# Taking the modulation's steps two together at every second place of a two-layer diffusion trunk

## The chip, the cores and the metric

The kernel runs on one core of one Trainium2 chip. The time is that of the device, in microseconds (us), for one execution; the median of several runs is compared.

## What is computed

Two layers of a diffusion trunk over 512 latent and 256 context tokens of 1024 features, all in 32-bit floats. Each layer has a SwiGLU block, a block of four parallel mixers, and a second SwiGLU block. Before and after each block the stream is scaled and shifted by vectors that depend on the condition alone, the modulation: nine vectors of 1024 values a layer and condition.

```python
m_l = (jax.nn.silu(c) @ w_mod[l] + b_mod[l]).reshape(b, N_MOD, d).transpose(1, 0, 2)[:, :, None, :]
m_c = (jax.nn.silu(c_ctx) @ w_mod[l] + b_mod[l]).reshape(N_MOD, 1, 1, d)

h_lat = h_lat + 0.5 * m_l[2] * swiglu(modulate(rms_norm(h_lat, g_ffn1[l]), m_l[0], m_l[1]),
                                      w1_gate[l], w1_up[l], w1_down[l])
z_lat = split_in(modulate(rms_norm(h_lat, g_mix[l]), m_l[3], m_l[4]) @ w_in[l])
...
h_lat = h_lat + m_l[5] * (jnp.concatenate([o_a, o_b, o_c, o_d], axis=-1) @ w_out[l])
h_lat = h_lat + 0.5 * m_l[8] * swiglu(modulate(rms_norm(h_lat, g_ffn2[l]), m_l[6], m_l[7]),
                                      w2_gate[l], w2_up[l], w2_down[l])
```

The context tokens (h_ctx, with m_c) go through the same blocks up to the last layer's mixers.

## The kernel before

Features lie on the 128 partitions and tokens on the free axis; the stream `h` stays on the chip (8 tiles of 128 features, 768 tokens). Every product is done in three passes on operands that are split into a high and a low part (`mm3`, L162: weights low by tokens high, high by low, high by high). A weight block of 128 x 512 comes from the memory into one of four `raw` buffers (`load`, L152, on SyncE's queue, SP) and is split by a ScalarE copy (L133) and a VectorE subtraction (L134) into `wh` and `wl` (`unit`).

The two SwiGLU blocks of a layer (`ffn`) go through the 22 hidden tiles in six chunks of 4, 2, 4, 4, 4 and 4. The first chunk is done by plain products (`first_pairs`, `plain`), the others by Strassen-Winograd over pairs of hidden tiles (`gate_up`: 7 products of 12 matmuls for the gate, m = 0, then 7 for the up part, m = 1). After a chunk's hidden tiles its part of the down product is added to `h` (`down`). Between them lie the mixers (`mixer`): input projection, two convolutions, and an attention stage that runs as a pipeline over units (scores and softmax, transposed weights, values), and then the output projection (`out_proj`).

The modulation is computed as filler between these products. `mod_group` is a generator for four blocks of 256 columns of `w_mod`. Its step k loads row block k (128 rows, 1024 columns, 512 KB) into the next of two buffers `mraw` (L176) and multiplies it with the 32 columns of `sc`, which hold silu of the two conditions (L179: four products of 128 x 32 by 128 x 256, each into its own 32 partitions of the bank `pmod`). After the eighth step ScalarE copies the sums (L184), TensorE transposes them twice (L186), and VectorE adds the bias (L195). The first two groups run at the start, from 16 buffers of their own (`i`). The other 16 groups, 128 steps, stand in `self.filler`. `fill(n)` takes n steps; it is called

- in the SwiGLU blocks of layer 0 (`FILLS`, L50, is 1 there and 0 in layer 1): after each gate or up half of a plain hidden tile (L371), after a hidden tile of the first pair (L400), before each half of a Strassen pair (L458), and after each chunk (L579). The call after a chunk and that before the next chunk's first half follow each other with no product between them;
- once for each unit of the attention pipeline (L1026) and for each column tile of the output projection (L1056), in both layers;
- by `need` and by the first chunk's end, if a part of the modulation is wanted that is not there yet (L209, L532).

I call each such call a place. The order on each engine's queue is set by the framework's scheduler, which takes the program's order with some parts moved ahead (`rise`); it may put other instructions between those of a step.

Of the kernel before, what the change touches and what calls it, by code (L numbers as in the profile page):

```python
# [33 lines left out]
# column tiles of the input projection, in order  # L34
T_CFA, T_CFG, T_KV, T_QA, T_QB, T_WQ, T_WK, T_WV, T_SC = 0, 2, 4, 5, 16, 6, 8, 9, 10

# small per-layer vectors: name -> (offset, width)
# [9 lines left out]
class K:  # L47
# [9 lines left out]
    def __init__(self, tc, ctx, a, out):  # L57
        self.tc, self.nc, self.a, self.out = tc, tc.nc, a, out
        self.const = ctx.enter_context(tc.tile_pool(name="const", bufs=1))
        psum = ctx.enter_context(tc.tile_pool(name="psum", bufs=1, space=bass.MemoryType.PSUM))  # L60
        ct = self.ct
        self.raw = deque(ct(f"raw{i}", (P, 1024)) for i in range(self.N_RAW))
        self.mraw = deque(ct(f"mraw{i}", (P, 1024)) for i in range(self.N_MRAW))
        self.wr = deque((ct(f"wh{i}", (P, 512), F32R), ct(f"wl{i}", (P, 512), F32R)) for i in range(self.N_W))
        # PSUM: two banks, and six that each phase cuts for itself
        self.mod_ps = psum.tile([P, 512], F32, name="pmod")
        self.one = psum.tile([P, 512], F32, name="pone")
        self.filler, self.found, self.open = iter(()), set(), False
        self.n = 0
# [4 lines left out]
    # ---- buffers: handed out and given back in program order  # L74
# [4 lines left out]
    @contextmanager  # L79
    def area(self, name, side="left"):  # L80
        """A phase's buffers: each in a pool of its own, so that it waits only for the users of its own bytes."""
        with ExitStack() as st:
            def take(n, w, dt=F32):
                ts = deque()
                for _ in range(n):
                    u = self.uid(name)
                    pool = st.enter_context(self.tc.tile_pool(name=u, bufs=1, side=side, reuse_waits="tile"))
                    ts.append(pool.tile([P, w], dt, name=u))
                return ts
            yield take  # L90

    def psum(self, st, n, w):
        """n pieces of PSUM, each in a pool of its own."""
        ts = deque()
        for _ in range(n):
            u = self.uid("ps")
            pool = st.enter_context(self.tc.tile_pool(name=u, bufs=1, space=bass.MemoryType.PSUM, reuse_waits="tile"))
            ts.append(pool.tile([P, w], F32, name=u))
        return ts
# [19 lines left out]
    def rise(self, n):  # L119
        """Work that the scheduler is to take as if it came n instructions earlier."""  # L120
        return self.tc.high_priority(n) if n else nullcontext()
# [5 lines left out]
    # ---- exact two-part split: x = hi + lo, each of 12 significant bits  # L127
# [13 lines left out]
    def unit(self, src, neg=False):  # L141
        """A split [parts, <= 512] block of weights."""
        hi, lo = self.turn(self.wr)
        p, w = src.shape[0], src.shape[-1]
        hi, lo = hi[:p, :w], lo[:p, :w]
        with self.rise(self.P_UNIT):
            self.split(hi, lo, src, neg)
        return hi, lo
# [6 lines left out]
    def mm3(self, ps, w, x, start, stop):  # L155
        """ps += w^T x for split operands, each [K, M] / [K, N]; N is cut at PSUM's banks."""
# [7 lines left out]
    # ---- modulation vectors  # L164
    def mod_group(self, l, blocks):
        """Two pairs of neighbouring blocks of 256 columns of silu(c) @ w_mod, for both conditions; one step a row block."""
# [39 lines left out]
    def need(self, l, part):  # L206
        """Has what is left of a part of the modulation computed."""
        while not {(l, 4 * part + j) for j in range(4)} <= self.found:
            self.fill()  # L209
# [5 lines left out]
    def norm_gain(self, l, part, ks=(0, 4)):  # L215
        """g * (1 + scale), both conditions."""
# [15 lines left out]
    # ---- norms  # L232
    def segs(self, a, b):
        """Token range [a, b) by condition."""
        return [(i, max(a, s), min(b, e)) for i, (s, e) in enumerate(((0, SEQ), (SEQ, TOK))) if max(a, s) < min(b, e)]

    def sumsq(self, k, a, b):
        """Adds the squares of h[k] to the running sum of this norm."""
# [10 lines left out]
    def sums(self, ps, tiles, n):  # L249
        """The sum over partitions and tiles, on all partitions."""  # L250
# [6 lines left out]
    def rsqrt(self, out, x, scale):  # L257
        """1 / sqrt(scale * x + eps)"""
# [3 lines left out]
    def spread(self, ps, rc):  # L262
        """A row of values by token on all partitions, from columns of values by token."""
# [3 lines left out]
    def inv_rms(self, ps, tiles, n, scale, j0=0):  # L267
        """1 / sqrt(scale * sum of squares + eps) on all partitions (in PSUM), found by token."""
# [9 lines left out]
    def rnorm(self, a, b, ps=None):  # L278
        """1 / rms(h) for tokens [a, b), on all partitions (in PSUM)."""
# [3 lines left out]
    def modulated(self, hi, lo, t, k, r, gain, l, part, a, b):  # L283
        """hi + lo = h[k] * gain * r + shift for tokens [a, b)."""
# [14 lines left out]
    # ---- SwiGLU. The gate and up products go by Strassen-Winograd over two column tiles,  # L299
    # two halves of the features and two halves of the tokens.  # L300
    def token_operands(self, X, hn, r, gain, l, part, half, kk):
        """Half of the features of the modulated norm of half of the tokens, split: B11 and B21, or B12 and B22."""
# [7 lines left out]
    def token_sums(self, X, hn):  # L310
        """T1 = B12 - B11, T2 = B22 - T1, T3 = B22 - B12, T4 = T2 - B21, split."""
# [24 lines left out]
    def half_load(self, idx, rs, f, m, kk):  # L336
        """Half of the features of the gate's (m = 0) or the up product's (m = 1) column tile f."""
# [8 lines left out]
    def whole(self, ps, w, x, hn, start, stop):  # L346
        """ps += a whole product over half of the features."""
# [4 lines left out]
    def hidden(self, g, j, hn, pss):  # L352
        """silu(gate) * up, split, for half j of the tokens."""
# [8 lines left out]
    def plain(self, idx, f, X, g, hn, fills):  # L362
        """The split hidden tile f by plain products."""
        pss = [[self.banks.popleft() for _ in range(2)] for _ in range(2)]
        for m in range(2):
# [5 lines left out]
            self.fill(fills)  # L371
# [3 lines left out]
    def first_pairs(self, idx, X, g, hn, norm, operands, fills, start):  # L375
        """The first four hidden tiles by plain products, while the operands are being made."""
# [16 lines left out]
        def product(f, j, kk):  # L393
# [4 lines left out]
            if kk == 1:  # L398
                self.hidden(g[f], j, hn, (pss[f, 0, j], pss[f, 1, j]))
                self.fill(fills)  # L400

        steps = self.STEPS if start else ((0, 0, (0, 1), ()), (0, 1, (), (0, 1)), (1, 0, (0, 1), ()), (1, 1, (), (0, 1)))
        for j, kk, lower, upper in steps:
            if kk == 0:
                r[j] = norm(j)
                if start and j == 0:
                    # both halves' norms are in use at a time
# [16 lines left out]
    def gate_up(self, idx, f, X, g, hn, fills):  # L424
        """g[0], g[1]: the split hidden tiles f and f + 1."""
# [11 lines left out]
        def ready(m, i, j, c):  # L437
            """c: tile i, token half j of the gate (m = 0) or up (m = 1) product."""
# [18 lines left out]
        for m, M in enumerate(mats):  # L457
            self.fill(fills)  # L458
# [35 lines left out]
    def ffn(self, l, which, part, n, cuts, fills, start=None):  # L494
        """cuts: token ranges in which the last chunk is finished;
        start: for the first of all, what gives the norms, and the weights that have been loaded."""
# [3 lines left out]
        with ExitStack() as st:  # L500
# [18 lines left out]
            for ci, nf in enumerate(F_CHUNKS):  # L519
# [18 lines left out]
                def down(i, w, j0, ranges):  # L538
                    """Column tile i over token ranges; w: its weights from column j0 on."""
# [36 lines left out]
                else:  # L576
                    if ci == 0:
                        self.token_sums(X, hn)
                    self.fill(fills)  # L579
                f0 += nf  # L580

    # ---- rotary embedding on partitions [p0, p1), latent tokens
# [14 lines left out]
    def dw_conv(self, y, u, w, taps, bias, segs):  # L597
        """y[t] = bias + sum_j w[:, j] u[t + j - taps // 2], zeros outside of each segment."""
# [18 lines left out]
    # ---- the four mixers; returns the 8 split tiles that the output projection reads  # L617
    def mixer(self, l, n, st):
        """n: tokens whose output is wanted (TOK, or SEQ in the last layer)."""
# [11 lines left out]
        # modulated norm, by stream  # L631
# [9 lines left out]
        def proj_parts(tiles, ranges, m=P):  # L641
            """Column tiles of the input projection, token range by token range."""
# [18 lines left out]
        # conformer: u = a * sigmoid(g), then a depthwise convolution spread over the other projections  # L661
# [18 lines left out]
        # kv latent  # L680
# [8 lines left out]
        # q latent (two tiles) and the shared rotary key  # L689
# [8 lines left out]
        # 1 / rms of the q latent, by token  # L698
# [14 lines left out]
        # window q, k, v  # L713
# [14 lines left out]
        # ---- attention  # L728
# [21 lines left out]
        # attention runs as a pipeline over units: scores and softmax; transposed weights; values  # L750
        po = self.one

        def transposed(blocks, res):
            """blocks: pairs of [128, 128] sources; [128, 512] split tiles of two pairs each."""
# [12 lines left out]
        # windowed attention with sink: units of 128 queries and one key head (two query heads)  # L767
# [6 lines left out]
        class Window:  # L774
# [6 lines left out]
            def softmax(w):  # L781
# [20 lines left out]
                # -max(scale * scores, sink)  # L802
# [31 lines left out]
        # latent attention: units of 256 queries of a head  # L834
# [48 lines left out]
        def mla_query(ps, c, m, wa, wb):  # L883
            """Columns [c, c + m) of the query projection."""
# [3 lines left out]
        def mla_rotary(h, wa, wb):  # L888
            """The rotary parts of the queries of heads h and h + 1, split, in rows that the query latent leaves free."""
# [42 lines left out]
        def window_operands():  # L932
            # a head's two parts above each other: one product sums two passes
# [27 lines left out]
        # short conv: b * conv(c * x); the first head of the latent attention starts beside it  # L961
# [35 lines left out]
        for i in range(len(units) + lv):  # L997
# [28 lines left out]
            self.fill()  # L1026
# [8 lines left out]
    def out_proj(self, l, o, gate, n):  # L1035
# [5 lines left out]
        def part(i, ranges):  # L1041
# [14 lines left out]
            self.fill()  # L1056
# [31 lines left out]
    def run(self, ctx):  # L1088
        nc, a, ct = self.nc, self.a, self.ct
        # constants and small vectors  # L1090
# [29 lines left out]
        with self.area("i") as init:  # L1120
            # keeps the place of the next phase's first buffers
# [42 lines left out]
        # final norm  # L1164
# [46 lines left out]
def _lay(inp):  # L1211
    """Layout only: transposes, permutations and packing of the inputs."""
# [3 lines left out]
    def fm(v):  # [n] -> [128, n/128]  # L1216
        return np.ascontiguousarray(v.reshape(-1, P).T)

    def lhs(w):  # [L, K, M] -> [L, M/128, 128, (K/128)*128]: one block per column tile
# [10 lines left out]
    # down projections: [128, chunk][column tile][row tile][128]  # L1230
# [6 lines left out]
    # input projection: columns by tile  # L1237
# [8 lines left out]
    # query projection: the heads' plain parts, then their rotary parts  # L1246
# [43 lines left out]
```

## Time and profile before

| | |
|---|---|
| median of 3 runs | 2734.28 us (2730.88 to 2735.37) |
| profiled execution, span from its first to its last instruction | 2729.7 us |
| profiled execution, time outside the span | not given apart; the median of the runs is 4.6 us above the span |
| TensorE busy | 2687.2 us (98% of the span) |
| VectorE, ScalarE, GpSimd busy | 1998.7, 1108.8, 65.5 us |
| transfers | 254.83 MB, 93 GB/s on average |
| modulation steps in the filler | 128 loads of 512 KB, 1024 matmul records on L179 |

Of the span, about 50 to 590 us are layer 0's first SwiGLU, up to 750 the head of its mixers, up to 905 its attention, up to 985 its output projection, up to 1500 its second SwiGLU. Layer 1 has its first SwiGLU up to 2050, its mixers up to 2316, its output projection up to 2360 and its second SwiGLU to the end.

How to read it: PE is TensorE's matmul, PEld its weight load, DVE VectorE, ACT ScalarE, POOL GpSimd, SPq SyncE's queue, which issues the loads. Matmul records have modelled ends and overlap, so the distance from one start to the next tells what a product costs, not the duration of its record. A product of 32-bit operands that are not rounded (L179) shows as two records.

### The profile page before, as it was taken

What the parts mean: (1) busy time and instruction counts of PE and PEld (TensorE: products, weight loads), DVE (VectorE), ACT (ScalarE), POOL (GpSimd) and SP (SyncE); (2) the same over time, 40 slices, a digit from 0 to 9 for tenths busy, and PEclk for the clock granted to TensorE, in tenths of its full rate; (3) what the DMA queues carried; (4) which work ended last, traced back from release to release, by engine and by line L of the source; (5) the groups of instructions that cost most, each with busy time, mean ns of one, the idle gap of its engine ahead of it and who ended that gap; (6) DMA issues with size and microseconds to landing.
All of it is one profiled execution on the core that took longest, in us unless ns stands there. A gap on an engine that the chain in (4) does not pass through costs nothing.

```text
span 2729.7 us, 41155 instructions
## 1 busy us (share of the span) xinstructions
PE 2687.2 (98%) x16292; PEld 2458.7 (90%) x16292; DVE 1998.7 (73%) x3884; ACT 1108.8 (41%) x2096; POOL 65.5 (2%) x88
## 2 busy tenths in 40 slices
PE   7999999999999999999999999999999999999998
PEld 5999999988876899999999999999998877899998
DVE  5777666779785476767667867776678785698887
ACT  4333323343375342333234523343244375444444
POOL 0000000000022000000000000000000021000000
PEclk9999999999999999999999999999999999999999
DMA  7323222321123342323223132222222122423322
GB/s 269 108 101 100 79 96 90 108 83 57 55 78 93 109 139 93 101 93 103 83 85 124 48 100 70 63 79 60 63 85 99 58 78 78 138 94 98 104 93 78
DMA packets 78241, 254.83 MB, mean 93 GB/s; under 512 B 8672, under 2 KB 14048, under 8 KB 77792
## 3 DMA queue, kind: packets, MB, share of 16 engines
q1 hardware_dynamic: 78048, 252.21, 28.7%
q8 instruction: 127, 2.08, 0.3%
q14 instruction: 66, 0.54, 0.1%
HBM read 250.08 MB, written 2.10 MB: 92 GB/s over the span
## 4 chain that ended last, share of the span: by engine, by line
PE 94%; DVE 4%; DMA 1%; ACT 1%; issue 1%; POOL 0%; DVEq 0%; SPq 0%; POOLq 0%; ACTq 0%
PE ps L162 73%; PE pone L162 10%; PE pmod L179 3%; PE pmod L162 3%; PE ps L595 1%; PE ps L793 1%; PE ps L798 1%; DVE r L134 0%; DMA raw<-in_w_gu 0%; DVE sm L852 0%; PE ps L796 0%; DMA mraw<-in_w_mod 0%; DVE wl L134 0%; PE ps L272 0%; PE pone L272 0%
## 5 line engine op out<-in xcount | busy, mean ns | idle before, releaser
L162 PE MATMUL ps<-x,wh 128*128 128x384 f32 (+1 forms) x3064 | 748.9, 329 | 0.0
L162 PEld LDWEIGHTS ps<-x,wh 128*128 128x128 f32 x3064 | 542.7, 188 | 0.1
L162 PE MATMUL ps<-x,wl 128*128 128x384 f32 (+1 forms) x1532 | 506.1, 331 | 0.0
L133 ACT ACTIVATE wh<-raw 128x512 fp32r<-128x512 f32 (+1 forms) x445 | 278.3, 626 | 486.9 <-PE ps L162 336.3
L134 DVE TENSOR_TENSOR wl<-raw,wh 128x512 fp32r<-128x512 f32 (+1 forms) x445 | 305.2, 687 | 121.9 <-ACT wh L133 119.1
L162 PE MATMUL ps<-t,wh 128*128 128x384 f32 (+2 forms) x1488 | 385.2, 341 | 0.3 <-DVE t L134 0.3
L162 PE MATMUL ps<-r,wh 128*128 128x512 f32 (+7 forms) x1432 | 355.5, 350 | 0.3 <-DVE r L291 0.3
L296 DVE SCALAR_TENSOR_TENSOR h<-ps,hg,h 128x256 f32<-128x256 f32 (+3 forms) x404 | 186.8, 506 | 186.6 <-PE ps L162 186.1
L162 PEld LDWEIGHTS ps<-x,wl 128*128 128x128 f32 x1532 | 287.6, 188 | 12.9 <-issue 10.7
L162 PEld LDWEIGHTS ps<-t,wh 128*128 128x128 f32 x1488 | 269.2, 188 | 7.2 <-DVE t L134 0.5
L133 ACT ACTIVATE wh<-t 128x512 fp32r<-128x512 f32 x217 | 136.0, 629 | 337.1 <-PE ps L162 201.9
L162 PEld LDWEIGHTS ps<-r,wh 128*128 128x128 f32 (+3 forms) x1432 | 236.4, 184 | 36.1 <-DVE r L291 1.5
L450 DVE TENSOR_TENSOR t<-t,ps 128x384 f32<-128x384 f32 (+1 forms) x422 | 217.2, 520 | 52.6 <-PE ps L162 50.2
L162 PE MATMUL ps<-t,wl 128*128 128x384 f32 (+2 forms) x744 | 253.4, 342 | 1.6 <-ACT t L133 1.6
L162 PE MATMUL ps<-r,wl 128*128 128x512 f32 (+5 forms) x716 | 225.1, 355 | 2.4 <-ACT r L290 1.3
L134 DVE TENSOR_TENSOR wl<-t,wh 128x512 fp32r<-128x512 f32 x217 | 149.1, 689 | 95.2 <-ACT wh L133 95.0
L133 ACT ACTIVATE t<-t 128x384 fp32r<-128x384 f32 (+2 forms) x247 | 130.2, 536 | 208.9 <-DVE t L444 100.7
L162 PE MATMUL ps<-x,t 128*128 128x384 f32 (+1 forms) x1308 | 204.4, 310 | 0.0
L162 PEld LDWEIGHTS ps<-x,t 128*128 128x128 f32 x1308 | 194.4, 188 | 0.0
L162 PE MATMUL ps<-t,t 128*128 128x384 f32 (+2 forms) x948 | 188.9, 345 | 0.0
L162 PEld LDWEIGHTS ps<-t,t 128*128 128x128 f32 x948 | 165.5, 188 | 10.9 <-issue 1.2
L134 DVE TENSOR_TENSOR t<-t,t 128x384 fp32r<-128x384 f32 (+2 forms) x247 | 137.4, 568 | 25.4 <-ACT t L133 25.0
(215 smaller groups left out, 3711.0 us busy)
## 6 DMA issues: line engine op xcount, KB each, us to landing
raw<-in_w_gu SPq DMA_DIRECT2D x160, 512.0 KB, 3.8
mraw<-in_w_mod SPq DMA_DIRECT2D x128, 512.0 KB, 4.0
raw<-in_w_dn SPq DMA_DIRECT2D x88, 512.0 KB, 3.7
raw<-in_w_in SPq DMA_DIRECT2D x34, 512.0 KB, 3.3
raw<-in_w_out SPq DMA_DIRECT2D x20, 512.0 KB, 3.4
i<-in_w_mod SPq DMA_DIRECT2D x32, 256.0 KB, 6.0
raw<-in_w_gu SPq DMA_DIRECT2D x32, 256.0 KB, 3.5
h<-in_h SPq DMA_DIRECT2D x4, 768.0 KB, 6.6
```

The costliest lines, as they stand in the source:

```text
L133: self.nc.scalar.activation(hi, x, AF.Copy)
L134: self.nc.vector.tensor_tensor(out=lo, in0=x, in1=hi.bitcast(F32), op=ALU.subtract)
L162: self.nc.tensor.matmul(ps[:, c:e], a, b[:, c:e], start=start and i == 0, stop=stop and i == 2)
L179: nc.tensor.matmul(ps[32 * j:32 * j + 32, :256], self.sc[:, k, :], r[:, j * 256:(j + 1) * 256], start=k == 0, stop=k == KD - 1)
L296: nc.vector.scalar_tensor_tensor(out=self.h[:, k, s:e], in0=ps[:, s - a:e - a], scalar=gate[:, k, i:i + 1], in1=self.h[:, k, s:e], op0=ALU ...
L450: eng.tensor_tensor(out=out, in0=p, in1=q, op=op)
L595: self.nc.tensor.transpose(out, in_, self.ident)
L793: nc.tensor.matmul(ps[:, c0:SEQ], a, b[:, kc], start=i == 0, stop=False)
L798: nc.tensor.matmul(ps[:, SEQ:TOK], a, b[:, SEQ:], start=i == 0, stop=i == 1)
```

## The change

A new function `spot` takes the place of `fill` at all places named above but `need` and the first chunk's end: it notes the steps owed and takes them when two or more have come together. So the first of two places does nothing and the second takes two steps. With `FILLS` 0 nothing is owed.

```diff
-        self.filler, self.found, self.open = iter(()), set(), False
+        self.filler, self.found, self.open, self.owed = iter(()), set(), False, 0
...
     def fill(self, n=1):
         for _ in range(n):
             next(self.filler, None)
 
+    def spot(self, n=1):
+        self.owed += n
+        if self.owed > 1:
+            self.fill(self.owed)
+            self.owed = 0
...
     def plain(self, idx, f, X, g, hn, fills):
...
-            self.fill(fills)
+            self.spot(fills)
...
     def first_pairs(self, idx, X, g, hn, norm, operands, fills, start):
...
-                self.fill(fills)
+                self.spot(fills)
...
     def gate_up(self, idx, f, X, g, hn, fills):
...
-            self.fill(fills)
+            self.spot(fills)
...
     def ffn(self, l, which, part, n, cuts, fills, start=None):
...
-                    self.fill(fills)
+                    self.spot(fills)
...
     def mixer(self, l, n, st):
...
-            self.fill()
+            self.spot()
...
     def out_proj(self, l, o, gate, n):
...
-            self.fill()
+            self.spot()
```

The lines below `spot` have numbers higher by 7 in the changed kernel: L162 is L169 there, L179 L186, L176 L183, L152 L159.

How the order on the queues moves is shown at three places. In the names, `x` are token operands, `wl` and `wh` split weights, `ps` and `pone` banks of sums, `mraw_65` and `mraw_66` the two buffers of the modulation, `sc` the condition.

**TensorE, layer 0's first SwiGLU, fourth chunk.** Before, at the border between the gate half and the up half of the chunk's first pair, and at the border to its second pair:

```order
L162 MATMUL ps_382<-x_530,wh_67 128x384
L162 MATMUL ps_382<-x_526,wh_67 128x384
L179 MATMUL pmod<-mraw_65,sc 32x256 x4
L162 MATMUL ps_390<-x_486,wl_70 128x384
L162 MATMUL ps_390<-x_490,wh_69 128x384
```

```order
L162 MATMUL ps_382<-x_530,wh_69 128x384
L162 MATMUL ps_382<-x_526,wh_69 128x384
L179 MATMUL pmod<-mraw_66,sc 32x256 x4
L162 MATMUL ps_390<-x_486,wl_72 128x384
L162 MATMUL ps_390<-x_490,wh_71 128x384
```

Now, at the same two borders:

```order
L169 MATMUL ps_382<-x_526,wl_68 128x384
L169 MATMUL ps_382<-x_530,wh_67 128x384
L169 MATMUL ps_382<-x_526,wh_67 128x384
L169 MATMUL ps_390<-x_486,wl_70 128x384
L169 MATMUL ps_390<-x_490,wh_69 128x384
```

```order
L169 MATMUL ps_382<-x_530,wh_69 128x384
L169 MATMUL ps_382<-x_526,wh_69 128x384
L186 MATMUL pmod<-mraw_65,sc 32x256 x4
L186 MATMUL pmod<-mraw_66,sc 32x256 x4
L169 MATMUL ps_390<-x_486,wl_72 128x384
```

The first border has no step any more, and the second has both, one behind the other.

**SP's queue, the loads around the same chunk** (`in_w_gu` gate and up weights, `in_w_dn` down weights). Before:

```order
L152 DMA raw_63<-in_w_gu 128x1024
L176 DMA mraw_66<-in_w_mod 128x1024
L176 DMA mraw_65<-in_w_mod 128x1024
L152 DMA raw_64<-in_w_gu 128x1024
L152 DMA raw_61<-in_w_gu 128x1024
L176 DMA mraw_66<-in_w_mod 128x1024
L152 DMA raw_62<-in_w_gu 128x1024
L152 DMA raw_63<-in_w_dn 128x1024
L176 DMA mraw_65<-in_w_mod 128x1024
L152 DMA raw_64<-in_w_dn 128x1024
L152 DMA raw_61<-in_w_dn 128x1024
L176 DMA mraw_66<-in_w_mod 128x1024
```

Now:

```order
L159 DMA raw_63<-in_w_gu 128x1024
L183 DMA mraw_65<-in_w_mod 128x1024
L183 DMA mraw_66<-in_w_mod 128x1024
L159 DMA raw_64<-in_w_gu 128x1024
L159 DMA raw_61<-in_w_gu 128x1024
L183 DMA mraw_65<-in_w_mod 128x1024
L183 DMA mraw_66<-in_w_mod 128x1024
L159 DMA raw_62<-in_w_gu 128x1024
L159 DMA raw_63<-in_w_dn 128x1024
L159 DMA raw_64<-in_w_dn 128x1024
L159 DMA raw_61<-in_w_dn 128x1024
L183 DMA mraw_65<-in_w_mod 128x1024
```

The weight loads have kept their order; two modulation loads now stand together between them where there was one at each of two points.

**TensorE, layer 0's attention stage, windowed units** (`f` and `r` are attention operands, `ident` the identity of a transpose). Before, two places in a row:

```order
L595 MATMUL ps_6337<-ident,f_4941 128x128
L179 MATMUL pmod<-mraw_65,sc 32x256 x4
L162 MATMUL pone<-f_4872,r_5033 64x256
L162 MATMUL pone<-f_4884,r_5029 64x256
L162 MATMUL pone<-f_4872,r_5029 64x256
```

```order
L798 MATMUL ps_5069<-r_4997,r_5053 128x256
L162 MATMUL pone<-f_4880,r_5029 64x256
L179 MATMUL pmod<-mraw_66,sc 32x256 x4
L595 MATMUL ps_6333<-ident,f_4953 128x128
L595 MATMUL ps_6337<-ident,f_4953 128x128
```

Now:

```order
L602 MATMUL ps_6332<-ident,f_4936 128x128
L186 MATMUL pmod<-mraw_65,sc 32x256
L169 MATMUL pone<-f_4867,r_5028 64x256
L169 MATMUL pone<-f_4879,r_5024 64x256
L169 MATMUL pone<-f_4867,r_5024 64x256
```

```order
L805 MATMUL ps_5064<-r_4992,r_5048 128x256
L169 MATMUL pone<-f_4875,r_5028 64x256
L186 MATMUL pmod<-mraw_65,sc 32x256 x3
L186 MATMUL pmod<-mraw_66,sc 32x256 x4
L602 MATMUL ps_6328<-ident,f_4948 128x128
```

Here the scheduler has put the first product of the pair's first step at the earlier point, and the other seven at the later one.

## Rows read from the trace of the kernel before

**Rows 1.** The page: engine totals, and the chain that ended last by engine.

```profile
PE 2687.2 (98%) x16292; PEld 2458.7 (90%) x16292; DVE 1998.7 (73%) x3884; ACT 1108.8 (41%) x2096; POOL 65.5 (2%) x88
...
PE 94%; DVE 4%; DMA 1%; ACT 1%; issue 1%; POOL 0%; DVEq 0%; SPq 0%; POOLq 0%; ACTq 0%
```

**Rows 2.** Windows: stretch, its length, each engine's busy time, clock, DMA share, GB/s.

```profile
50.00:560.00 510.00, 510.00 (x3021) 490.83 (x3020) 364.08 (x690) 177.99 (x324) 0.00 (x0) 1.00 0.31 99
750.00:912.00 162.00, 158.52 (x1070) 114.94 (x1070) 108.12 (x246) 105.95 (x239) 35.75 (x48) 0.99 0.28 85
1615.00:2050.00 435.00, 435.00 (x2461) 433.01 (x2460) 310.63 (x572) 148.99 (x266) 0.00 (x0) 1.00 0.23 69
2190.00:2316.00 126.00, 123.38 (x800) 91.14 (x801) 88.42 (x188) 82.63 (x180) 28.96 (x32) 0.99 0.23 72
```

**Rows 3.** TensorE's timeline (start, us, records) around one step, layer 0's second SwiGLU.

```profile
1253.61 0.34 PE L162 MATMUL ps<-x,wl 128*128 128x384 f32 x1
...
1254.14 0.34 PE L162 MATMUL ps<-x,wl 128*128 128x384 f32 x1
1254.32 0.52 PE L162 MATMUL ps<-x,wh 128*128 128x384 f32 x2
1254.77 0.64 PE L179 MATMUL pmod<-mraw,sc 128*32 128x256 f32 x8
1255.33 0.45 PE L162 MATMUL ps<-x,wl 128*128 128x384 f32 x1
...
1255.97 0.34 PE L162 MATMUL ps<-x,wl 128*128 128x384 f32 x1
```

**Rows 4.** TensorE's timeline around two steps at a border between chunks, same stage.

```profile
1238.14 0.69 PE L162 MATMUL ps<-t,t 128*128 128x384 f32 x3
1238.75 1.07 PE L179 MATMUL pmod<-mraw,sc 128*32 128x256 f32 x16
1239.75 0.44 PE L162 MATMUL ps<-x,wl 128*128 128x384 f32 x1
...
1240.39 0.34 PE L162 MATMUL ps<-x,wl 128*128 128x384 f32 x1
```

**Rows 5.** TensorE's timeline at two points of layer 0's attention stage.

```profile
865.82 0.95 PE L162 MATMUL pone<-f,r 128*64 128x256 f32 x6
866.70 0.64 PE L179 MATMUL pmod<-mraw,sc 128*32 128x256 f32 x8
867.27 0.44 PE L595 MATMUL ps<-ident,f 128*128 128x128 f32 x2
...
890.58 1.05 PE L179 MATMUL pmod<-mraw,sc 128*32 128x256 f32 x10
891.56 0.70 PE L798 MATMUL ps<-r,r 128*128 128x256 f32 x2
```

**Rows 6.** Waits of 750 to 912 us: engine, line, for whom; us, times, longest.

```profile
PE ps L162 <- ACT f L855: 1.6, 2, 1.3
```

**Rows 7.** Waits of SP's queue over the whole span.

```profile
SPq L152 <- DVE t L450: 881.1, 90, 18.8
...
SPq L176 <- PE pmod L179: 498.4, 110, 19.8
```

**Rows 8.** TensorE's timeline, end of layer 0's output projection and the next stage's start.

```profile
978.85 0.64 PE L179 MATMUL pmod<-mraw,sc 128*32 128x256 f32 x8
...
983.85 1.07 PE L179 MATMUL pmod<-mraw,sc 128*32 128x256 f32 x16
985.45 0.58 PE L162 MATMUL ps<-x,x 128*128 128x384 f32 x2 [0.53 <-ACT x L290]
```

**Rows 9.** Modulation loads, issue to landing: two issued together (1093 us); one alone (1255 us).

```profile
DMA to landing us min/median/max: 4.1/4.9/5.8
...
mraw<-in_w_mod SPq DMA_DIRECT2D x1, 512.0 KB, 4.3
```

## Prediction

> **What bounds the kernel now.** I read the totals and the chain of waits first. TensorE is busy for 2687.2 of 2729.7 us and the chain that ended last runs through it for 94% [rows 1]. The windows by stage then tell where it has slack. In the first SwiGLU stage it is busy in every one of 510.00 us, in the second layer's first SwiGLU in 435.00 of 435.00, in the two attention stages in 158.52 of 162.00 and 123.38 of 126.00 [rows 2]. The granted clock is 1.00 (2.4 GHz) or 0.99 in them. So a microsecond taken out of TensorE's queue in these stages is a microsecond off the end, and the question is what one modulation step takes out of that queue, alone and behind another.
>
> The timeline has both forms in the kernel as it is. A place (where the filler is called) with **one step** shows as 8 records (4 products of two records each); where the end of a chunk and the start of the next stand side by side, two steps already come together, as 16 records. I call an unbroken stretch of modulation products on TensorE a **visit**.
>
> - One step: the products around it come in threes (one with the low weights, two with the high ones), and a three takes 1254.14 - 1253.61 = 0.53 us. Around the visit two threes take 1255.97 - 1254.14 = 1.83 us in place of 1.06, so the visit costs **0.77 us** [rows 3].
> - Two steps together: three products start at 1238.14 and the next would start at 1238.67; it starts at 1239.75, 1.08 late, and the three behind it takes 0.64 in place of 0.53, 0.11 more. The visit costs **1.19 us** [rows 4].
>
> Two visits of one step cost 1.54 us, one visit of two costs 1.19: **0.35 us less for each visit that goes away**. What is dear is going in and coming out (the gap before the first record, the longer way to the next product and its slow start), not the step, which adds 1.19 - 0.77 = 0.42.
>
> **The change, part by part.** *How many visits go.* The number of steps stays 128. Counted in the two orders that are printed, the steps of these 16 groups make 128 visits before (a coincidence: some hold two steps, and the scheduler cuts others into pieces) and 91 after. By stage, before and after: SwiGLU 1 of layer 0 28 and 17; its attention 31 and 25; its output projection 10 and 5; SwiGLU 2 26 and 16; the stretch into layer 1 5 and 5; layer 1's mixer head 4 and 4, attention 18 and 16, output projection 6 and 3.
>
> *SwiGLU and output projections: 11 + 5 + 10 + 3 = 29 visits.* Both sides of a visit are the 384- or 512-column products of rows 3 and 4, so 29 x 0.35 = **10.2 us**. The inside of a chunk goes from three visits to one or two; the double at every border between chunks stays, so the place where hidden tiles and down products meet keeps what it has.
>
> *Attention: 6 + 2 = 8 visits.* The neighbours are short products and transposes. A step of 8 records takes 0.57 us from its first record to the next product (866.70 to 867.27), 10 records of two steps take 0.98 (890.58 to 891.56) [rows 5]. Two visits of 0.57 against one of 0.98 is 0.16 saved at least; with the gap on going in, as in rows 3, up to 0.35. I take 0.25, since transposes stand nearer together than the products of rows 3 and lose less: 8 x 0.25 = **2.0 us**, with 1.3 and 2.8 as ends.
>
> *Places that lose their step.* About half of the places have nothing now, and the next half tile's products come 0.77 us sooner. Its weights must be split by then (ScalarE, then VectorE). The nearest row is layer 1's first SwiGLU, the same code with no step at any place: TensorE idles for nothing in 435 us [rows 2]. I cost it at 0 there. In the attention stages such a place may leave a wait open that a step covered; the largest wait on the softmax's exponentials is 1.6 us in two times [rows 6]. I cost it at 0 and keep 0 to 5 us for the range.
>
> *The loads.* Each step loads a row block of 512 KB into one of two buffers, on SP's queue, and that load waits until the step two before it has been multiplied. SP already waits 498.4 us for that, 110 times, and 881.1 us in one group alone for weight buffers [rows 7]. Both buffers of a pair now come free together, so two loads go out behind each other, once for two places, with the weight loads behind them. Set against the times of before, no weight load then stands behind a modulation load whose buffer frees later than that weight load went out anyway: weight buffers hold SP longer. The tightest pair is the end of layer 0's output projection: one visit at 978.85, the next at 983.85 [rows 8], with two loads between them where there was one. Two loads issued together landed after 4.1 and 5.8 us, one alone after 4.3 [rows 9]. So the second may come up to 1.5 us late; TensorE waits 0.53 us for ScalarE right behind this visit [rows 8], which hides part. I cost it at **0.5 us**, with 0 and 1.5 as ends.
>
> On this one place the Trainium skill speaks against the change: by "Trainium Kernel Development and Optimization", section Key Constraints, all transfers run on the same 16 DMA engines and interleave, so two loads at once should each take about twice as long. At 2 x 4.3 = 8.6 us the wait would be some 4 us and the sum 8.2 in place of 11.7; the trace's 5.8 us for the later of a pair agrees only in part.
>
> *Elsewhere.* VectorE, ScalarE and GpSimd have the same operations. No part of the modulation comes later than it is wanted: pairs end with their groups of 8 steps, and each group closes within a few products of where it did.
>
> **The sum.** 10.2 + 2.0 - 0.5 = 11.7 us off the profiled span of 2729.7, so 2718.0. The three timed runs have a median 4.6 us above that span (2734.28); I take that distance to stay: **2722.6 us**, 0.43% faster. About 0.2% (5.5 us) is what a measurement of this kernel can tell from no change.
>
> **Rivals.**
> - *Attention gives it back* (2728.8 to 2739). Some 18 places there lose their step. If at each the softmax chain leaves TensorE waiting as long as a visit took (0.57), 10.3 us return and 2733 is left. For it: these are the only stages with idle time, and the scheduler puts their products in another order. Against it: the named wait is 1.6 us [rows 6]. Within 0.2%, 13%.
> - *Slower: the weights come late behind pairs.* The later load of a pair lands 5.8 - 4.1 = 1.7 us after the first [rows 9], and a weight load behind both lands later by as much. In the two SwiGLU stages of layer 0 some 31 visits are pairs; if TensorE waited 1.7 us at the 20 new ones, that is 34 us, and 2722.6 + 34 = 2757. It decides as soon as a weight's lead, from landing to its first split, is under 1.7 us; half of that wait is enough for no gain. Against it: the 11 doubles of now have weight loads behind them too, and TensorE does not idle there [rows 2]. 7%.
> - *The pairs don't come about.* The scheduler may take steps apart, as it does in attention, where a first product goes ahead and the other seven follow. If nothing is gained there the time is 2724.6, inside the forecast's range.
> - *Less of a saving than the double shows*, because it stands at a border between chunks: with 0.16 (rows 5) at all 37 the gain is 5.9, less 0.5, and the time 2728.9. 5%, 2 of them faster and 3 no change.
>
> **Chances and range.** The forecast 75%, the rivals 13, 7 and 5%: so faster 75 + 2 = 77%, no measurable change 13 + 3 = 16%, slower 7%. The forecast's own range: 29 x 0.35 + 2.8 = 13.0 off at best gives 2721.3, and runs spread over 4.5 us, so it starts at 2718; at the other end 5 us come back in attention and 1.5 at the loads, which gives 2726.6, and half of the rivals' cases below 2734 reach to 2730.5. So 2718 to 2730.5 holds 8 in 10.
>
> **What would show it.** In the changed profile: inside the SwiGLU chunks visits of 16 records, cost 1.19 as in rows 4, and none of 8; a chunk pair of layer 0 shorter by 3 x 0.35; TensorE's busy share there still 100%; its idle time named "issue" ahead of modulation products falling with the number of visits; attention no longer than 162 and 126 us. Wrong would be: TensorE waiting for a modulation load or a split weight in SwiGLU, a lone visit cheaper than 0.77 where it still stands, or attention stages that grew.

## The result and the profile after

The changed kernel took 2718.15 us (median of 5 runs, 2715.30 to 2723.11), the kernel before 2735.37 us (median of the 5 runs beside it). The ratio is 0.9941, with a 95% interval of 0.9929 to 0.9953: 0.47 to 0.71% faster. A second measurement gave 0.9941 again (0.9929 to 0.9954; 6 runs against 23). The forecast was 2722.6 us and 0.43%.

The two profiles show less than the medians: spans of 2729.7 us before and 2721.3 us after. The profiled execution of before is one of the faster of its kernel, with a mean granted clock of 0.995, and that of after the second slowest of 11, at 0.994; what that is worth is measured below (e1). So I read the stages, not the spans.

The windows by stage of the changed kernel (columns as in [rows 2]):

```profile
50.00:560.00 510.00, 509.96 (x3026) 496.09 (x3025) 364.51 (x692) 178.23 (x325) 0.00 (x0) 1.00 0.31 99
750.00:905.00 155.00, 151.72 (x1029) 111.30 (x1028) 105.19 (x239) 98.81 (x230) 35.25 (x48) 0.98 0.28 89
985.00:1490.00 505.00, 505.00 (x3016) 491.87 (x3016) 361.70 (x697) 177.15 (x323) 0.00 (x0) 1.00 0.31 100
2185.00:2310.00 125.00, 123.60 (x807) 92.03 (x808) 89.05 (x189) 83.03 (x182) 28.97 (x32) 1.00 0.23 73
```

TensorE is still busy all through the SwiGLU stages: nothing took the place of what went. In the attention stages it idles 3.3 and 1.4 us, no more than before [rows 2].

TensorE's timeline inside a chunk of layer 0's second SwiGLU, where one step stood before [rows 3]:

```profile
1278.98 0.34 PE L169 MATMUL ps<-x,wl 128*128 128x384 f32 x1
...
1279.51 0.34 PE L169 MATMUL ps<-x,wl 128*128 128x384 f32 x1
1279.69 0.52 PE L169 MATMUL ps<-x,wh 128*128 128x384 f32 x2
1280.13 1.07 PE L186 MATMUL pmod<-mraw,sc 128*32 128x256 f32 x16
1281.13 0.44 PE L169 MATMUL ps<-x,wl 128*128 128x384 f32 x1
...
1281.76 0.34 PE L169 MATMUL ps<-x,wl 128*128 128x384 f32 x1
```

An undisturbed three takes 0.53 us; the two around the visit take 1281.76 - 1279.51 = 2.25 in place of 1.06. So the visit costs 1.19 us, what the double at the border between chunks cost before [rows 4], and no single step is left inside the chunks.

What the idle time of TensorE's weight load (PEld) ahead of modulation products was put down to, whole span (us, times); first the kernel before:

```profile
  issue: 27.0, 111
```

and the changed kernel:

```profile
  issue: 18.0, 77
```

That is 0.24 and 0.23 us a time, and the number of times falls with the visits, as forecast. Most of it overlaps with products that still run: going by start times, a visit begins only 0.10 us late (1254.77, where 1254.67 was due [rows 3]).

SP's queue in the changed kernel (compare [rows 7]):

```profile
SPq L159 <- DVE t L457: 874.5, 87, 18.7
...
SPq L183 <- PE pmod L186: 372.4, 75, 25.8
```

Fewer waits for modulation buffers, 75 in place of 110, the longest longer (25.8 us for 19.8), less in total. The end of layer 0's output projection, TensorE's timeline (compare [rows 8]):

```profile
975.52 1.07 PE L186 MATMUL pmod<-mraw,sc 128*32 128x256 f32 x16
...
980.96 1.07 PE L186 MATMUL pmod<-mraw,sc 128*32 128x256 f32 x16
982.55 1.13 PE L169 MATMUL ps<-x,x 128*128 128x384 f32 x5 [0.53 <-ACT x L297]
```

and the landing of the two loads between these visits:

```profile
DMA to landing us min/median/max: 3.7/4.1/4.5
```

TensorE waited for neither; the 0.53 us for ScalarE is the same wait as before. Over all 128 modulation loads the median landing rose from 4.0 to 4.4 us and the longest from 6.6 to 7.7.

### The profile page after: what moved, and what is told of

It reads as the page before. It is cut to its first block, busy times and chain, and to the rows that moved or that the text cites. A ratio compares the mean times of both kernels' runs of the same rounds, so it can differ in the third digit from the quotient of the medians.

```text
span 2721.3 us, 41161 instructions
## 1 busy us (share of the span) xinstructions
PE 2679.1 (98%) x16292; PEld 2467.3 (91%) x16292; DVE 1998.2 (73%) x3884; ACT 1108.1 (41%) x2096; POOL 65.5 (2%) x88
## 5 line engine op out<-in xcount | busy, mean ns | idle before, releaser
L169 PE MATMUL ps<-x,wh 128*128 128x384 f32 (+1 forms) x3064 | 748.3, 329 | 0.0
L169 PEld LDWEIGHTS ps<-x,wh 128*128 128x128 f32 x3064 | 542.6, 188 | 0.1
L169 PE MATMUL ps<-x,wl 128*128 128x384 f32 (+1 forms) x1532 | 504.6, 330 | 0.0
L169 PE MATMUL ps<-t,wh 128*128 128x384 f32 (+2 forms) x1488 | 385.6, 341 | 0.2 <-DVE t L141 0.2
L169 PE MATMUL ps<-r,wh 128*128 128x512 f32 (+7 forms) x1432 | 355.6, 350 | 0.3 <-DVE r L298 0.3
L169 PEld LDWEIGHTS ps<-x,wl 128*128 128x128 f32 x1532 | 287.6, 188 | 7.5 <-issue 3.7
L169 PEld LDWEIGHTS ps<-t,wh 128*128 128x128 f32 x1488 | 269.2, 188 | 7.0 <-DVE t L141 0.4
L169 PEld LDWEIGHTS ps<-r,wh 128*128 128x128 f32 (+3 forms) x1432 | 235.6, 184 | 36.5 <-DVE r L298 1.5
L169 PE MATMUL ps<-t,wl 128*128 128x384 f32 (+2 forms) x744 | 253.1, 341 | 1.3 <-ACT t L140 1.3
L169 PE MATMUL ps<-r,wl 128*128 128x512 f32 (+5 forms) x716 | 223.3, 353 | 2.0 <-ACT f L862 1.2
L169 PE MATMUL ps<-x,t 128*128 128x384 f32 (+1 forms) x1308 | 204.1, 309 | 0.0
L169 PEld LDWEIGHTS ps<-x,t 128*128 128x128 f32 x1308 | 194.1, 188 | 0.0
L169 PE MATMUL ps<-t,t 128*128 128x384 f32 (+2 forms) x948 | 188.9, 345 | 0.0
L169 PEld LDWEIGHTS ps<-t,t 128*128 128x128 f32 x948 | 165.4, 188 | 10.9 <-issue 1.2
```

What stands on the lines that cost most here:

```text
L169: self.nc.tensor.matmul(ps[:, c:e], a, b[:, c:e], start=start and i == 0, stop=stop and i == 2)
```

## The experiments

The times of e1 to e4 are set against 23 runs of the kernel before on the same chip (median 2732.87 us); e5 to e9 are single runs on other chips, made for their profiles. Since the granted clock turned out to move single runs by more than some of the effects, each run of e1 to e4 is also compared with the runs of before that had the same mean clock (the mean of the granted clock over the run, as a share of 2.4 GHz). That clock is given to 0.001, which is worth 2.3 us (below), so these comparisons are good to 1 us or so.

The profiles allow a second comparison. I take the products other than the steps in their order, go from one of them to the one with the same number in another kernel, and take off half of the time that lies at 1.2 GHz. This is an estimate, since it supposes that TensorE sets the pace there. From 50 to 2700 us the three profiles of before come to 2643.2, 2642.9 and 2640.6 us in this way, and the three of the change (one from the first measurement, e1 and e8) to 2629.1, 2629.8 and 2630.0.

**e1, the change again.**

> The changed kernel once more, beside the kernel before. Theory (visits): 37 visits fewer at about 0.33 us is 12 us, whatever the clock does; what the medians showed beyond that (17 us) is the granted clock of single runs. Then runs of both kernels with the same mean clock differ by 11 to 13 us, and the time of either falls with the clock by some 2.5 us for each 0.001. Rival (something else was saved): at equal clocks the two differ by 16 us or more. Second rival (fewer half-clock windows because of the change): the changed kernel's mean clock is higher than that of the kernel before by 0.002 on average.

Median 2718.31 us (6 runs). With the 5 of the first measurement there are 11 runs:

| mean clock | before, us (runs) | changed, us (runs) | difference |
|---|---|---|---|
| 0.993 | 2735.83 (6) | 2723.62 (1) | 12.2 |
| 0.994 | 2732.78 (6) | 2721.52 (2) | 11.3 |
| 0.995 | 2731.39 (7) | 2718.38 (3) | 13.0 |
| 0.996 | 2730.01 (1) | 2716.68 (4) | 13.3 |

At equal clock the change is worth 11 to 13 us, as the theory had it (12 to 14 by the six runs of e1 alone, and 12.6 by the means of the profiles), and each 0.001 of mean clock 2.3 us (before: 2738.31 at 0.992 in 3 runs, 2731.39 at 0.995). The first rival falls. The second is only partly right: the mean clock was 0.9939 over 23 runs of before and 0.9952 over 11 of the change, 0.0013 more, where the rival asked for 0.002. That is 3 us on top of the 12.

**e2, attention as before.**

```diff
                 out(4, oc[0])
-            self.spot()
+            self.fill()
```

> The change in the SwiGLU blocks and the output projections alone; the attention units take one step each as before. Theory: 29 of 37 visits go, so 10 us faster than before and 2 to 3 us slower than the full change. Rival (attention gives back): as fast as the full change or faster, since the attention stages then lose nothing. Second rival (attention brings the part beyond 12 us): 5 us or more slower than the full change.

Median 2730.12 us (12 runs), ratio 0.998 (0.997 to 0.999). At equal clock it is 8.1 us faster than before (2724.72 against 2732.78 at 0.994; 2730.21 against 2738.31 at 0.992), and 3 to 4 us slower than the full change (2724.72 against 2721.52 at 0.994; 2722.00 against 2718.38 at 0.995): between the theory's 2 to 3 and the second rival's 5. The first rival falls. By the profiles (this one and e9) it comes to 2632.0 us from 50 to 2700, 10.2 faster than before and 2.4 slower than the full change, as the theory had it. TensorE's records show 101 visits, 27 fewer than before: 0.30 us each. By medians it gains only 2.7 us, because its mean clock was 0.9926, lower than that of any other kernel here.

**e3, pairs in attention alone.**

```diff
 # in plain, first_pairs, gate_up, ffn:
-            self.spot(fills)
+            self.fill(fills)
 # in out_proj:
-            self.spot()
+            self.fill()
```

> The change in the attention units alone; the SwiGLU blocks and the output projections take one step at each place. Theory: 8 visits go, 2 to 3 us faster than before, hardly to be told from no change. Rival (attention gives back): 0 or slower by up to 10 us. Second rival: 5 us faster or more.

Median 2732.68 us (11 runs), ratio 0.9998 (0.9989 to 1.0006): no difference that can be told. At equal clock (0.992 to 0.995) it is 1.4, 1.4, 0.4 and 1.4 us faster, for 8 visits fewer. The rival (attention gives the gain back) and the second (5 us or more) fall. By equal clock the part is worth 1.1 us alone and 3 to 4 on top of the rest, where the theory had 2 to 3. The profiles show no such difference: the two attention stages together (750 to 905 and 2190 to 2316 us of before) are 3.1 us shorter in the change and 3.1 in e3, and e3 is 2.7 us shorter in all (one profile). With e2's 10.2 that makes 12.9, against 12.6 for the change. The scheduler orders the products of the attention stages anew in each of these kernels (in e2 they are 1.1 us shorter than before, though each unit takes one step); what each order costs is not shown.

**e4, four together in the SwiGLU blocks.**

```diff
-        if self.owed > 1:
+        if self.owed >= len(self.mraw):
...
             st.callback(setattr, self, "wr", wr)
+            if fills:
+                mr = self.mraw
+                self.mraw = deque(mr)
+                self.mraw.extend(tmp(2, 1024))
+                st.callback(setattr, self, "mraw", mr)
```

> As the change, but in layer 0's SwiGLU blocks four steps come together at every fourth place, with two more buffers for the row blocks there. Theory (a visit costs 0.34 us plus 0.43 for each step): visits of 32 records, each 0.77 + 3 x 0.43 = 2.06 us, and some 15 visits fewer than the change has, so 5 us faster than it. Rival (weights come late behind several loads in SP's queue): TensorE waits for split weights behind the visits, and the time is that of the change or above it.

Median 2716.78 us (5 runs), ratio to before 0.9931 (0.9918 to 0.9945). At equal clock it beats the change by 3.4, 4.6 and 4.1 us (2720.24 at 0.993, 2716.92 at 0.994, 2712.56 at 0.996). It has 85 visits, 6 fewer than the change and not 15: the theory's count was wrong, and its 5 us came near by luck. Six visits at 0.35 us make 2.1 us; where the other 2 come from is not shown (the one profile is 3.3 us shorter than those of the change from 50 to 2700). The price of a visit held. TensorE's timeline around a visit of four steps in layer 0's first SwiGLU (the two further buffers are named `t`):

```profile
320.48 0.34 PE L169 MATMUL ps<-x,wl 128*128 128x384 f32 x1
320.66 0.52 PE L169 MATMUL ps<-x,wh 128*128 128x384 f32 x2
321.10 1.07 PE L186 MATMUL pmod<-mraw,sc 128*32 128x256 f32 x16
321.99 1.05 PE L186 MATMUL pmod<-t,sc 128*32 128x256 f32 x16
322.97 0.44 PE L169 MATMUL ps<-x,wl 128*128 128x384 f32 x1
...
323.60 0.34 PE L169 MATMUL ps<-x,wl 128*128 128x384 f32 x1
```

323.60 - 320.48 = 3.12 in place of 1.06: the visit costs 2.06 us, the theory's number to the hundredth. Its windows by stage:

```profile
50.00:560.00 510.00, 510.00 (x3035) 500.39 (x3034) 366.38 (x695) 178.75 (x326) 0.00 (x0) 1.00 0.29 95
1000.00:1480.00 480.00, 480.00 (x2870) 468.54 (x2869) 340.11 (x643) 162.99 (x294) 0.00 (x0) 1.00 0.30 96
```

Even behind visits of four steps, with four loads to follow, TensorE waited for no weight. That is the hardest test of the slower rival here, and it fell. In the second SwiGLU the scheduler took four of the fours apart again (two steps, 8 to 11 products, two steps), which is one reason that so few visits went. It is the fastest version here.

**e5, the steps over all 128 columns.**

```diff
-    N_RAW, N_MRAW, N_W = 4, 2, 5
+    N_RAW, N_MRAW, N_W = 4, 2, 4
...
             for j in range(4):
-                nc.tensor.matmul(ps[32 * j:32 * j + 32, :256], self.sc[:, k, :], r[:, j * 256:(j + 1) * 256], ...)
+                s = 96 + 128 * k - 32 * j
+                nc.tensor.matmul(ps[:, :256], self.sc[:, s:s + P], r[:, j * 256:(j + 1) * 256], ...)
...
-        self.sc = ct("sc", (P, KD, 32))
+        self.sc = ct("sc", (P, 1120))
...
```

> The kernel before (one step at a place, two at the borders between chunks), but each of a step's four products uses all 128 columns of the array: the condition's two columns stand among zeros, and all four add into the same bank. One buffer pair of split weights fewer, for room; so the time of the whole tells nothing, and the rows around single and double visits tell it. The steps themselves become longer, since the four products no longer stand beside each other. Theory A (what a visit costs beyond its steps is the switch between products of 32 and of 128 columns): twice a single visit minus a double one, 0.35 us before, falls under 0.1 us. Theory B (it is the switch between rounded and unrounded 32-bit operands, or the drain of any visit): it stays at 0.25 us or more.

One run: 2846.2 us; the steps are much dearer. TensorE's timeline around a double step at a border between chunks and then around a single one (layer 0's first SwiGLU, with steps at places as before):

```profile
163.71 0.33 PE L162 MATMUL ps<-t,wl 128*128 128x384 f32 x1
163.89 0.51 PE L162 MATMUL ps<-t,wh 128*128 128x384 f32 x2
164.23 3.62 PE L180 MATMUL pmod<-mraw,sc 128*128 128x256 f32 x16
167.50 0.53 PE L162 MATMUL ps<-x,wl 128*128 128x384 f32 x1
167.86 0.52 PE L162 MATMUL ps<-x,wh 128*128 128x384 f32 x2
```

```profile
266.81 0.34 PE L162 MATMUL ps<-x,wl 128*128 128x384 f32 x1
266.98 0.52 PE L162 MATMUL ps<-x,wh 128*128 128x384 f32 x2
267.34 1.89 PE L180 MATMUL pmod<-mraw,sc 128*128 128x256 f32 x8
268.88 0.53 PE L162 MATMUL pone<-x,wl 128*128 128x384 f32 x1
269.24 0.51 PE L162 MATMUL pone<-x,wh 128*128 128x384 f32 x2
```

Without a visit the product that follows would start at 164.23 and 267.34, and the one behind it 0.18 later. The double puts them back by 167.50 - 164.23 = 3.27 and by another 0.18, 3.45 together; the single by 1.54 and 0.18, 1.72. Twice the single minus the double is -0.01 us, where it was 0.35 with 32 columns. The operands are as unrounded as before and their neighbours as rounded, so theory B falls. These visits are no exceptions: over all that stand between products of 384 columns the medians are 0.76 us (51 single) and 1.19 (11 double) before, 1.72 (43) and 3.44 (11) here.

One rival is left: in e5 the four products of a step also run one after another, where they stood side by side. The change's own trace decides it. Near 57 us the scheduler has left one product of a step alone (two records), with nothing beside it:

```profile
56.69 0.52 PE L169 MATMUL ps<-x,wl 128*128 128x384 f32 x2
57.14 0.62 PE L186 MATMUL pmod<-mraw,sc 128*32 128x256 f32 x2
57.69 1.66 PE L169 MATMUL ps<-x,x 128*128 128x384 f32 x8
59.19 0.52 PE L169 MATMUL ps<-x,wh 128*128 128x384 f32 x2
```

The product behind it would have started at 57.04 and starts 0.65 late; the eight take 1.50 us in place of 1.41. So one lone product costs 0.74 us, nearly as much as a step of four (0.77), and a product over 128 columns costs 0.43 (1.72 / 4). The other 0.31 us come with one product, as some 0.34 come with four. **The price of a visit is the switch between products of 128 and of 32 columns.** The Trainium skill, in "TensorEngine Tiling (Array Packing)", section Key Properties, says that changing the tiling mode, not just the tile, drains TensorE. The trace agrees: some 0.35 us for there and back.

**e6 to e9, where the clock falls.**

> The kernel before, unchanged, for a second profile of it. Theory (chance): the stretches at half clock lie at the same few points of the program as in the first profile and in those of the other kernels (near 50, 650, 750, 900, 2110, 2270 to 2290 and 2450 us, each behind a stretch in which TensorE idles or does products of a few columns), and which of these points falls to half clock differs from run to run of the same kernel. Rival (the order decides): this profile has its stretches at the same places as the first one, 655, 904, 2119 and 2286 us.

> The same once more: by theory another choice among the same points, by the rival the same places again.

> The changed kernel, a third profile. By theory again a choice among the same points, not that of its first two profiles; by the rival those of its first two profiles, where they agree.

> The kernel with pairs outside attention, a second profile; its mean clock over 12 runs was 0.0026 below that of the full change. By the rival it has stretches at half clock at 750 and 2450 us again, as in its first profile, and these make the difference; by theory it has another choice of points.

Times were 2731.37, 2731.31, 2720.64 and 2724.58 us. By the granted clock in the traces, TensorE ran at 1.2 GHz from these points on (us), for 3.4 us unless 6.8 is noted:

| kernel | points between 100 and 2700 us |
|---|---|
| before | 655, 904, 2119, 2286 |
| before (e6) | 655, 904, 2119, 2286 |
| before (e7) | 587, 655, 884, 904, 2119, 2457 |
| changed | 651 (6.8), 896 (6.8), 2112, 2450 |
| changed (e1) | 652, 895, 2267, 2287 |
| changed (e8) | 652, 894, 1491, 2109, 2447 |
| attention as before (e2) | 650 (6.8), 749, 2278, 2449 (6.8) |
| attention as before (e9) | 648 (6.8), 747 (6.8), 901, 2273, 2280 |
| pairs in attention alone (e3) | 657, 753 (6.8), 903 (6.8), 1507, 2125, 2463 |
| four together (e4) | 649, 2103 |

Both are right in part. A few points are in every profile of a kernel (650 and 900 in before and the change), and 2267 to 2287 and 2450 come and go between runs of the same kernel, as does 2110 in the change. One seems to belong to the order of the products: near 750 the clock fell in both profiles of the kernel with attention as before and in that of e3, and in none of the three of before, the three of the change and that of e4. Windows around that point, first e2 and then the kernel before:

```profile
745.30:748.70 3.40, 1.44 (x10) 1.07 (x10) 2.67 (x7) 2.96 (x4) 0.21 (x1) 1.00 0.01 2
748.70:752.10 3.40, 3.40 (x12) 1.70 (x11) 2.60 (x5) 2.38 (x6) 1.57 (x2) 0.51 0.02 5
```

```profile
746.30:749.70 3.40, 1.73 (x11) 1.31 (x10) 3.31 (x9) 2.17 (x2) 0.00 (x0) 1.00 0.02 6
749.70:753.10 3.40, 3.36 (x20) 2.46 (x21) 2.13 (x7) 3.20 (x9) 1.80 (x2) 1.00 0.02 5
```

In e2 TensorE was busy for 1.44 of 3.40 us ahead of the fall. The kernel before has a stretch with 1.73 of 3.40 there, and its clock stayed; what decides between the two is not shown. Half the clock for 3.4 to 6.8 us is 0.0006 to 0.0012 of the mean over the run (an estimate), which can be part of the 0.0013 by which e2's mean lies below that of before. Why the change's mean is 0.0013 above that of before stays open: three profiles of each show no point that it lost for good, and one that it gained. At 48 to 50 us all three of the change have such a stretch, and none of before.

## Why the prediction was right, and where it was off

- **The bound.** Right: TensorE's queue sets the end, and what left it in the SwiGLU stages left the end. In the first profiles, from the first product of layer 0's second SwiGLU to a product 3371 products further it was 985.45 to 1601.46 before and 982.55 to 1594.56 after: 4.0 us less for 10 visits, where 0.35 each made 3.5. By the means of the three profiles of each kernel, the two SwiGLU stages of layer 0 and both output projections are 9.6 us shorter together, where 10.2 was forecast.
- **The price of a visit.** 0.77, 1.19 and 0.42 for a further step were right, and e4 stretches them to four steps (2.06). I called it going in and coming out; e5 and the lone product show that it is the switch of column width. Why that is dear the prediction had left open.
- **The count.** 91 visits, as the order showed.
- **Attention, 2.0 us.** The sign was right and the size is uncertain, with ends of 1.3 and 2.8 forecast: 1.1 alone (e3) and 3 to 4 on top of the rest (e1 against e2) by equal clock, 3.1 for the two stages by the profiles of the change and of e3. The rows I priced it from [rows 5] stood among neighbours that the scheduler then moved.
- **The loads, 0.5 us off.** It was 0: the later load of the tightest pair landed after 4.5 us, not 5.8 [rows 9]. The doubling that sharing the engines would give did not come there, nor over all loads (median 4.0 us before, 4.4 after).
- **Places without a step.** Nothing, as in layer 1's first SwiGLU [rows 2]; this was the step on which the slower rival hung.
- **The sum.** 11.7 us forecast; 12.3 is the middle of the 11.3 to 13.3 at equal clock. The medians differ by more, 17.2 us in the first measurement and 14.6 in the second, and the clock is 3 us of that by the estimate under e1. One sum of the range was wrong: with 5 us back in attention and 1.5 in place of 0.5 at the loads, 2722.6 becomes 2728.6, not 2726.6. The end of 2730.5 does not rest on it.
- **The absolute time** was 4.5 us too high. That the measured median lies inside the range, 0.15 us above its lower end of 2718.0, is luck: 5 of the 11 runs of the change lie below it. The step that failed is "I take that distance to stay", the 4.6 us from the profiled span to the median. In each run listed with its span the time is 1.8 us above it. The other 2.8 us would be the clock of the runs that made the median (theirs is not on record), and the change's runs got 0.0013 more of it than those of before.

Of the rivals, that attention gives it back and that the weights come late are refuted by e3 and e4; that the pairs don't come about held in part in attention alone, where 49 visits became only 41; a smaller saving than the double shows is refuted by the doubles inside the chunks.

## What to carry to other kernels

On a queue that is always full, as TensorE's here, a small product of another column width costs twice: itself (0.42 us for a step of four), and the change of width on the way in and out (0.35 us). Price it by the start-to-start distances of its neighbours, once for a lone visit and once for a visit of two, and the difference tells what gathering is worth before anything is built. Four steps together were better here than two, but look in the trace at which of them the scheduler left together, and count every buffer that they read from. When the effect is half a percent, compare runs at equal granted clock, and stage by stage.

## What was not expected of the hardware

The mean granted clock explains most of the spread between runs of the same program: 2.3 us for each 0.001, with 0.991 to 0.997 seen. The stretches at 1.2 GHz are of more than one kind. Some come behind a stretch in which TensorE idles, as here in the changed kernel, layer 1's second SwiGLU:

```profile
2446.20:2449.60 3.40, 1.17 (x5) 0.99 (x6) 3.40 (x10) 1.26 (x4) 0.00 (x0) 1.00 0.02 6
2449.60:2453.00 3.40, 3.40 (x10) 2.65 (x9) 1.56 (x3) 0.00 (x0) 0.00 (x0) 0.50 0.88 292
```

TensorE was busy for 1.17 of 3.40 us, and then ran at half clock through 3.40 us. The kernel before has this wait too; its clock fell there in one profile of three. Others come while TensorE is busy all the time. Near 650 and 900 us, the points that every profile of before and of the change has, it does products with a result one or two columns wide. In the kernel before, 22 products of 128x1 start from 900.78 us on:

```profile
900.40:903.80 3.40, 3.40 (x36) 2.97 (x34) 0.86 (x2) 2.39 (x5) 0.00 (x0) 1.00 0.54 154
903.80:907.20 3.40, 3.40 (x17) 3.30 (x14) 0.02 (x1) 2.15 (x5) 0.00 (x0) 0.50 0.50 157
```

So a busy share of 100% in this view does not mean that the clock stays. Ahead of 2286 us TensorE was busy for 3.40 of 3.40 us as well, with results 128 to 384 wide; that is neither of the two kinds that e6's theory named, and why the clock falls there is not shown.
